# Output-weight parts moved to another pool, and the first stage's pools laid out anew, in a recurrence, attention and expert trunk on one core

## The chip, the cores and the metric

The kernel runs on one core of a Trainium2 chip. TensorE (PE) multiplies matrices, its weight loads are shown apart as PEld; VectorE (DVE), ScalarE (ACT) and GpSimd (POOL) work on tiles; SyncE (SP) issues most DMAs. Each engine runs its own instructions in the order in which the program gives them, and waits for the others by semaphores. The metric is the device time of one execution in microseconds (us), the median of several runs. TensorE's granted clock has two levels here, 1.2 and 2.4 GHz, shown as 0.50 and 1.00.

## What is computed

A trunk of two layers on 256 tokens of width 1024: an RWKV7 layer with a dense SwiGLU, then forgetting attention with a mixture of 8 experts. The change lies in the first, whose time mixing is

```python
r, k, v = jnp.einsum('nbtd,nde->nbte', xs[:3], w_rkv)
...
def step(S, inp):
    r_t, w_t, k_t, v_t, kk_t, a_t = inp
    sa = jnp.einsum('bhij,bhj->bhi', S, -kk_t)
    S = (S * w_t[:, :, None, :] + sa[..., None] * (kk_t * a_t)[:, :, None, :]
         + v_t[..., None] * k_t[:, :, None, :])
    return S, jnp.einsum('bhij,bhj->bhi', S, r_t)
...
y = (y + bonus.reshape(B, T, D)) * g      # y: group norm of the scan's output
return y.astype(x.dtype) @ w_o
```

with 16 heads of 64, followed by `x = x + ...` and a dense stage `silu(u @ w_g) * (u @ w_u) @ w_down` of width 3584.

## The kernel before

Four stages follow each other: `rwkv()` (lines 387 to 1119), `ffn` (the dense stage, line 1122), `fox` and `moe`. Matrices are multiplied in three products: each operand is split into a rounded part and its rest (ACT casts `wh`, DVE subtracts to `wl`, lines 214 to 216), and `mm3` (lines 218 to 221) issues three matmuls.

**The first stage is cut into parts.** The 16 heads are two halves `nh` of 8. Per half: `project` multiplies the mixed inputs by the weights of k, r and v (line 639; v's second half is called the v-projection below); `operands`, `bkt` and `grams` make the scan's operands by chunks of 64 tokens; `solve(nh)` inverts the triangular matrices; `chain(nh, par)` steps the state through 4 chunks, in two parts `par` of four heads each; `finish(nh, t)` does the group norm and the gate for 128 tokens; `outp` multiplies by the output weights. A *group* of `outp` is six matmuls on one output weight and one `t`.

**A solve** writes its diagonal blocks to DRAM (`dU`, line 890) and reads them back turned (`U`, 897), substitutes in 30 steps of two DVE instructions (lines 907 and 909), then two memsets (912, 913), writes the result (`dW`, line 916) and reads it back (lines 921 to 923). Then for two halves `hf`: ACT copy `w11` (line 931), DVE transpose `x11` (933), 16 small matmuls `pB` (938), ACT copy `bsb`, 16 matmuls `pW` (944), ACT copy back. All these DMAs are on SP's queue.

**A chain step** is matmuls `cb` (line 972), ACT copy `rh` (980), matmuls `cc` (984), DVE copy (987), matmuls `ce` (993), two DVE operations (997, 998), matmuls into `cb` (1002) and ACT copy `yt` (1005). The last ones leave in time for the next step.

**`finish`** is three DVE operations (lines 1041 to 1043), ACT square (1046), DVE (1048, 1050), ACT root (1052), DVE (1054 to 1056), four PE transposes (1062), four DVE operations (1066), ACT cast `zh` (1072) and DVE `zl` (1074).

**The order is made by a planner.** The stage's instructions keep the order in which they are written, and `weave` (lines 423 to 496) decides it when the program is built. Every part is a generator that yields an engine and a cost before each piece; `weave` keeps a clock for each engine and goes on with the part whose next piece can start first. A part also waits for marks (`yield "W", ...`) and takes stock: "B" are PSUM banks, "U" small tiles, "Q" the tiles of pool `qpool`, given back by `free`. A rule on a mark or a stock so decides the order of all parts, on all engines.

**Weights.** `loads` brings the 24 weights of k, r, v and the 8 output weights, 512 KB each, on SP's queue through four raw tiles (line 606). `weights` splits those of k and the output weights (lines 630 and 632) into tiles `wh` and `wl` of pool `wsp`, which has two of each:

```python
if len(ns) >= OPT["sb"]:
    yield "W", ("used", ns[-OPT["sb"]])
```

so the split of an output weight waits until `outp` has used the one two before it. The pool `qpool` has 8 tiles of 4 KB per partition; four of them are stock, and hold at the end the recurrence operands `Q`, one for each `nh`, `t` and `par`.

**The dense stage's memory.** After `rwkv()` its pools are freed, and those of the later stages (lines 1667 to 1687) take the same addresses: `fn` (norm tiles, 24 KB per partition), `wraw` (three raw tiles of 8 KB), `wsph` (four of 8 KB), `wspl` (three of 8 KB). `Weights` streams the weights (line 181); it loads and splits ahead where its tiles are free, that is where the tiles of the first stage at the same addresses have been used for the last time. Before, `fn` lies on `rq`, `wraw` on `rq`, `rx` and `rm`, `wsph` on `rm`, `rws` and `ru`, `wspl` on `ru`.

Of the kernel before, what the change touches and what calls it, by code (L numbers as in the profile page):

```python
# [11 lines left out]
F32R = mybir.dt.float32r  # L12
# [95 lines left out]
def tile_trunk(ctx: ExitStack, tc: tile.TileContext, x, norm_g, final_g, mu, w_rkv, w0, w1, w2, a0, a1, a2,  # L108
# [277 lines left out]

    def rwkv():
        es = ExitStack()
        qpool = es.enter_context(tc.tile_pool(name="rq", bufs=8))
        xpool = es.enter_context(tc.tile_pool(name="rx", bufs=2))  # L390
        mpool = es.enter_context(tc.tile_pool(name="rm", bufs=2))
        wsp = es.enter_context(tc.tile_pool(name="rws", bufs=OPT["sb"]))
        upool = es.enter_context(tc.tile_pool(name="ru", bufs=OPT["nu"]))
        lpool = es.enter_context(tc.tile_pool(name="rl", bufs=2))
        wraw = es.enter_context(tc.tile_pool(name="rwr", bufs=4))
        U2 = lambda shape, name, dt=F32: upool.tile(shape, dt, name=name, tag="u")
        h3 = lambda a: a.rearrange("p (h d) -> p h d", d=HD)
        half = lambda c: slice(64 * (c % 2), 64 * (c % 2) + 64)
# [10 lines left out]
        def mark(*key):  # L409
            done[key] = now[0]  # L410

        def free(n, kind):

            stock[kind].extend([now[0]] * n)
# [201 lines left out]
        def weights():  # L616
            ns = []
            for i, key in enumerate(wkey):
                if key in OPT["whole"]:
                    yield "W", ("raw", i)  # L620
                    wts[i] = raw[i], None
                    mark("w", i)
                    continue
                if len(ns) >= OPT["sb"]:
                    yield "W", ("used", ns[-OPT["sb"]])
                ns.append(i)
                yield "W", ("raw", i)
                yield "A", cost_a(1024)
                hi, lo = (wsp.tile([128, 2, 512], F32R, name=nm, tag=nm) for nm in ("wh", "wl"))
                nc.scalar.copy(hi, raw[i])  # L630
                yield "V", cost_v(1024)
                nc.vector.tensor_tensor(lo, raw[i], hi.bitcast(F32), ALU.subtract)
                wts[i] = hi, lo
                mark("rawfree", i)
                mark("w", i)
# [317 lines left out]
        def chain(nh, par):  # L953
            g3 = lambda a: h3(a)[:, par:8:2, :]
            yield "W", ("v", nh)
            for c in range(4):
# [47 lines left out]
                yield "A", cost_a(256), "i"  # L1004
                nc.scalar.copy(g3(y)[half(c)], h3(pb[64:128, 0:256]))
                free(2, "B")
                mark("chain", nh, par, c)
                if last(2, "chain", nh, c):
                    free(3, "U")
# [68 lines left out]
        def outp():  # L1078
# [3 lines left out]
            for i in range(0, 8, 2):  # L1082
# [6 lines left out]
                for t, nh in ((0, 0), (1, 0), (0, 1), (1, 1)) if i < 6 else ((0, 0), (0, 1), (1, 0), (1, 1)):  # L1089
                    yield "W", ("w", n + i + nh)  # L1090
                    yield "P", 1.3
                    for j in range(2):
                        k = i + j
                        mm3(pw[t][nh], zh[k // 4, t][:, k % 4, :], zl[k // 4, t][:, k % 4, :],
                            wts[n + i + nh][0][:, j, :], wts[n + i + nh][1][:, j, :], k == 0, k == KB - 1)
                    if i == 6:
                        yield "V", cost_v(512), "i"
                        add_res(t, nh, pw[t][nh])
                    if t == 1:
                        mark("used", n + i + nh)  # L1100

        gnb = {}
        lwa = lora_w([(w1[0], 3, 0, 64), (a1[0], 4, 64, 64)], "lwa")
# [562 lines left out]
            rwkv()  # L1666
    wes = ExitStack()
    tpool = lambda name, bufs: tc.tile_pool(name=name, bufs=bufs, reuse_waits="tile")
    fpool = wes.enter_context(tpool("fn", 1))
    wraw = wes.enter_context(tpool("wraw", NRA))  # L1670
    specs = []
    if "ffn" in stages:
# [6 lines left out]
    wsp = [wes.enter_context(tpool("wsph", NWH)), wes.enter_context(tpool("wspl", NWL))]  # L1679
    W = Weights([wraw] * NRA, wsp, specs, 2)  # L1680
    W.load()
    mpool = wes.enter_context(tpool("mn", 1))
    wr = mpool.tile([128, KB, E], F32, name="wr")
    load_consts(mpool, C_MOE)
# [75 lines left out]
```

## Time and profile before

| | |
|---|---|
| median of 3 runs | 1637.76 us (1635.51 to 1640.74) |
| the profiled execution's own time | 1641.72 us |
| its span, first to last instruction | 1639.9 us |
| mean granted clock of PE | 0.962 |
| first stage, up to the dense stage's first matmul | 0 to 279.64 us |
| dense stage's first matmul to the end | 279.64 to 1639.9 us |

The profile is of one execution. A timeline row tells when an instruction started, how long it took, and, in brackets, how long its engine had stood idle before it and which instruction of which engine ended that wait. Rows of equal instructions that follow each other are drawn together (x16). In a table by windows the granted clock is a mean over the window: between 0.50 and 1.00 it changed within.

### The profile page before, as it was taken

The page shows a single profiled execution, that of the slowest core. Times are in us where ns is not written, and L with a number is a line of the kernel's source. Part 1 is how long each engine was busy: PE and PEld are TensorE (multiplying, and loading weights), DVE is VectorE, ACT ScalarE, POOL GpSimd, SP SyncE. Part 2 cuts the span into 40 slices and gives each one's busy share as a digit, 9 for nine tenths or more (in the row PEclk, how much of TensorE's full clock was granted, in tenths as well). Part 3 has the DMA queues.
Part 4 walks back from the last instruction along what each step waited for, and adds up shares of the span by engine and source line. Part 5 has one row for each costly group of instructions (what it writes and reads, how often), then busy time and mean ns, then how long its engine had stood idle before and what let it go on. Part 6 is the DMA issues. An engine that isn't in the chain of part 4 may idle for free.

```text
span 1639.9 us, 19904 instructions
## 1 busy us (share of the span) xinstructions
PE 1540.9 (94%) x7309; PEld 1208.2 (74%) x7309; DVE 1275.5 (78%) x1292; ACT 1088.5 (66%) x1092; POOL 176.8 (11%) x230
## 2 busy tenths in 40 slices
PE   5998998999999999999898999999999989989997
PEld 4664876888887886777666788888777667667886
DVE  6587657455536555589999998899799999999986
ACT  4533244444435664489888888787888889887884
POOL 0313010000000000001111111111011111111110
PEclk9997799999999998989999999999999999999999
DMA  5243133554565452369999999899899999999992
GB/s 176 89 110 106 34 104 118 202 204 163 198 196 172 155 180 78 139 262 399 409 403 401 373 395 353 335 394 349 330 382 406 402 403 391 397 402 408 406 359 101
DMA packets 156839, 446.19 MB, mean 272 GB/s; under 512 B 24128, under 2 KB 29296, under 8 KB 156704
## 3 DMA queue, kind: packets, MB, share of 16 engines
q1 hardware_dynamic: 105440, 262.95, 44.2%
q0 software_dynamic: 45920, 176.31, 28.0%
q10 hardware_dynamic: 5344, 5.07, 1.2%
q8 instruction: 91, 1.49, 0.4%
q14 instruction: 44, 0.36, 0.1%
HBM read 442.19 MB, written 2.11 MB: 271 GB/s over the span
## 4 chain that ended last, share of the span: by engine, by line
PE 43%; issue 27%; DMA 9%; DVE 8%; POOL 3%; ACT 3%; POOLq 0%; ACTq 0%; DVEq 0%; SPq 0%
DMA raw<-in_moe_w_gu_dram 9%; PE pgu L1492 8%; POOL raw L181 3%; PE acc L1492 3%; PE pgu L220 3%; PE pgu L221 3%; PE pgu L219 3%; DVE wl L216 3%; ACT wh L215 2%; PE acc L220 2%; PE acc L219 2%; PE acc L221 2%; PE pp L219 1%; PE pp L221 1%; PE pp L220 1%
## 5 line engine op out<-in xcount | busy, mean ns | idle before, releaser
L216 DVE TENSOR_TENSOR wl<-raw,wh 128x2048 fp32r<-128x2048 f32 x398 | 893.9, 2286 | 146.4 <-PE acc L220 35.3
L215 ACT CAST wh<-raw 128x2048 fp32r<-128x2048 f32 x398 | 752.9, 1918 | 272.2 <-PE pgu L221 51.4
L1492 PE MATMUL pgu<-wh,xg 128*128 128x512 f32 x1232 | 329.4, 400 | 1.5 <-issue 1.5
L1492 PEld LDWEIGHTS pgu<-wh,xg 128*128 128x128 f32 x1232 | 237.0, 194 | 52.3 <-issue 2.9
L1492 PE MATMUL pgu<-wl,xg 128*128 128x512 f32 x896 | 252.2, 403 | 10.7 <-DVE wl L216 7.8
L1492 PEld LDWEIGHTS pgu<-wl,xg 128*128 128x128 f32 x896 | 167.6, 192 | 68.2 <-DVE wl L216 35.0
L1492 PE MATMUL acc<-wh,hx 128*128 128x512 f32 x616 | 162.2, 395 | 0.0
L181 POOL DMA_DIRECT2D raw<-in_moe_w_gu_dram x112 | 80.0, 714 | 650.4 <-DVE wl L216 572.2
L1492 PEld LDWEIGHTS acc<-wh,hx 128*128 128x128 f32 x616 | 116.2, 191 | 23.6
L1492 PE MATMUL acc<-wl,hx 128*128 128x512 f32 x448 | 125.4, 401 | 4.5 <-DVE wl L216 2.0
L1492 PEld LDWEIGHTS acc<-wl,hx 128*128 128x128 f32 x448 | 82.6, 190 | 33.9 <-DVE wl L216 17.9
L219 PE MATMUL pgu<-wh,uh 128*128 128x512 f32 x224 | 89.3, 400 | 1.9 <-ACT wh L215 1.9
L220 PE MATMUL pgu<-wl,uh 128*128 128x512 f32 x224 | 88.1, 394 | 1.3 <-DVE wl L216 1.3
L221 PE MATMUL pgu<-wh,ul 128*128 128x512 f32 x224 | 88.1, 394 | 0.0
L181 POOL DMA_DIRECT2D raw<-in_moe_w_down_dram x56 | 39.5, 705 | 271.1 <-DVE wl L216 259.1
L1525 ACT CAST gc<-pgu 128x512 fp32r<-128x512 f32 x112 | 61.1, 594 | 0.0
L1492 PE MATMUL pgu<-gc,fold 128*128 128x512 f32 x70 | 30.9, 480 | 22.2 <-ACT gc L1525 21.9
L220 PEld LDWEIGHTS pgu<-wl,uh 128*128 128x128 f32 x224 | 42.6, 190 | 10.6 <-DVE wl L216 2.0
L219 PEld LDWEIGHTS pgu<-wh,uh 128*128 128x128 f32 x224 | 42.6, 190 | 10.6 <-ACT wh L215 2.1
L221 PEld LDWEIGHTS pgu<-wh,ul 128*128 128x128 f32 x224 | 42.6, 190 | 9.1
L219 PE MATMUL acc<-wh,hh 128*128 128x512 f32 x112 | 43.9, 392 | 0.0
L221 PE MATMUL acc<-wh,hl 128*128 128x512 f32 x112 | 43.7, 390 | 0.0
(361 smaller groups left out, 2013.9 us busy)
## 6 DMA issues: line engine op xcount, KB each, us to landing
raw<-in_moe_w_gu_dram SPq DMA_DIRECT2D x112, 1024.0 KB, 9.9
raw<-in_moe_w_gu_dram POOLq DMA_DIRECT2D x112, 1024.0 KB, 10.2
raw<-in_moe_w_down_dram SPq DMA_DIRECT2D x56, 1024.0 KB, 9.7
raw<-in_moe_w_down_dram POOLq DMA_DIRECT2D x56, 1024.0 KB, 9.6
raw<-in_ffn_w_gu_dram SPq DMA_DIRECT2D x28, 1024.0 KB, 5.5
raw<-in_fox_w_in_dram SPq DMA_DIRECT2D x16, 1024.0 KB, 5.7
raw<-in_ffn_w_down_dram SPq DMA_DIRECT2D x14, 1024.0 KB, 4.9
raw<-in_rwkv_w_rkv_dram SPq DMA_DIRECT2D x24, 512.0 KB, 4.3
```

The source lines that it names most:

```text
L181: (nc.gpsimd if self.nd >= N_EARLY and self.nd % 2 else nc.sync).dma_start(t, src)
L215: nc.scalar.copy(hi, src)
L216: nc.vector.tensor_tensor(lo, src, hi.bitcast(F32), ALU.subtract)
L219: nc.tensor.matmul(o, lh, rh, start=first, stop=False)
L220: nc.tensor.matmul(o, lh, rl, start=False, stop=False)
L221: nc.tensor.matmul(o, ll, rh, start=False, stop=last)
L1492: nc.tensor.matmul(o, l, r, start=first, stop=last, skip_group_check=True)
L1525: nc.scalar.copy(gc, p)
```

## The change

An output weight's `wh` and `wl` now come from `qpool`, in the place of two operand tiles. The split no longer waits for `used`; it takes two "Q" of stock. A "Q" is given back after each second step of a chain part, and two by `outp` after an output weight's last use. The pools of `rwkv` are created in another order, and `fn` after the weights' pools: now `wraw` lies on `rws` and `rx`, `wsph` on `rm` and `rwr`, `wspl` and `fn` on `ru`.

```diff
     def rwkv():
         es = ExitStack()
-        qpool = es.enter_context(tc.tile_pool(name="rq", bufs=8))
+
+        wsp = es.enter_context(tc.tile_pool(name="rws", bufs=OPT["sb"]))
         xpool = es.enter_context(tc.tile_pool(name="rx", bufs=2))
         mpool = es.enter_context(tc.tile_pool(name="rm", bufs=2))
-        wsp = es.enter_context(tc.tile_pool(name="rws", bufs=OPT["sb"]))
+        wraw = es.enter_context(tc.tile_pool(name="rwr", bufs=4))
         upool = es.enter_context(tc.tile_pool(name="ru", bufs=OPT["nu"]))
         lpool = es.enter_context(tc.tile_pool(name="rl", bufs=2))
-        wraw = es.enter_context(tc.tile_pool(name="rwr", bufs=4))
+        qpool = es.enter_context(tc.tile_pool(name="rq", bufs=8))
...
-                if len(ns) >= OPT["sb"]:
-                    yield "W", ("used", ns[-OPT["sb"]])
-                ns.append(i)
+                if key != "o":
+                    if len(ns) >= OPT["sb"]:
+                        yield "W", ("used", ns[-OPT["sb"]])
+                    ns.append(i)
                 yield "W", ("raw", i)
+                if key == "o":
+                    yield "Q", 2
                 yield "A", cost_a(1024)
-                hi, lo = (wsp.tile([128, 2, 512], F32R, name=nm, tag=nm) for nm in ("wh", "wl"))
+                hi, lo = ((wsp if key != "o" else qpool).tile([128, 2, 512], F32R, name=nm, tag=nm if key != "o" else "Q")
+                          for nm in ("wh", "wl"))
...
                 free(2, "B")
+                if c % 2 == 1:
+                    free(1, "Q")
                 mark("chain", nh, par, c)
...
                     if t == 1:
                         mark("used", n + i + nh)
+                        free(2, "Q")
...
-    fpool = wes.enter_context(tpool("fn", 1))
     wraw = wes.enter_context(tpool("wraw", NRA))
...
     W.load()
+    fpool = wes.enter_context(tpool("fn", 1))
```

The planner makes another order from it, from the end of the first solve to the start of the dense stage; from the dense stage's weights on the instructions are in the same order. Line numbers in the changed kernel are higher, by 5 from the weights on, and by 7 from `finish` on. Three places follow.

**SP, the second solve's DMAs and what follows** (`dU`, `U`, `dW`, `Mab` and `w` are the solve's; `raw` are weights). Before:

```order
L890 DMA dU_1256<-Mab 32x32x32 x2
L897 DMA U<-dU_1256 64x1024 x2
L916 DMA dW_1257<-W 1024x1x32 x2
L921 DMA Mab<-dW_1257 32x32x32
L922 DMA w_1594<-dW_1257 32x32x32
L923 DMA Mab<-dW_1257 32x32x32
L606 DMA raw<-in_rwkv_w_o_dram 128x2x512 x7
L181 DMA raw<-in_ffn_w_gu_dram 128x4x512 x28
```

With the change:

```order
L895 DMA dU_1256<-Mab 32x32x32 x2
L902 DMA U<-dU_1256 64x1024 x2
L607 DMA raw<-in_rwkv_w_o_dram 128x2x512 x3
L921 DMA dW_1257<-W 1024x1x32 x2
L607 DMA raw<-in_rwkv_w_o_dram 128x2x512
L926 DMA Mab<-dW_1257 32x32x32
L927 DMA w_1664<-dW_1257 32x32x32
L928 DMA Mab<-dW_1257 32x32x32
L607 DMA raw<-in_rwkv_w_o_dram 128x2x512 x2
L181 DMA raw<-in_ffn_w_gu_dram 128x4x512 x3
L607 DMA raw<-in_rwkv_w_o_dram 128x2x512
L181 DMA raw<-in_ffn_w_gu_dram 128x4x512 x25
```

Three output weights are now issued ahead of `dW`, one between `dW` and the reads that wait for it, and three of the dense stage's weights ahead of the last output weight.

**DVE, the end of the second solve's substitution** (`tm` and `W` are its steps; `VS`, `st` the first chain's). Before, its last steps and what follows:

```order
L907 TENSOR_TENSOR tm<-W,U 128x30
L909 TENSOR_TENSOR W<-W,tm 128x15x2
L907 TENSOR_TENSOR tm<-W,U 128x15
L909 TENSOR_TENSOR W<-W,tm 128x15
L912 MEMSET W 64x16
L913 MEMSET W 64x16
L1041 TENSOR_REDUCE gst<-yt 128x8
L1042 TENSOR_SCALAR gst<-gst 128x8
L1043 TENSOR_TENSOR yt<-yt,gst 128x512
L1048 TENSOR_TENSOR yt<-yt,gnb 128x512
```

With the change, a piece of its middle (the steps of 16 to 14 columns):

```order
L1061 RECIPROCAL gst<-gst 128x8
L1062 TENSOR_TENSOR yt<-yt,gst 128x512
L1063 TENSOR_TENSOR yt<-yt,v_1147 128x512
L912 TENSOR_TENSOR tm<-W,U 128x128
L914 TENSOR_TENSOR W<-W,tm 128x8x16
L992 COPY VS_1169<-cc 64x4x64
L912 TENSOR_TENSOR tm<-W,U 128x120
L914 TENSOR_TENSOR W<-W,tm 128x8x15
L637 TENSOR_TENSOR wl<-raw,wh 128x1024
L912 TENSOR_TENSOR tm<-W,U 128x126
L914 TENSOR_TENSOR W<-W,tm 128x9x14
L1073 SCALAR_TENSOR_TENSOR z<-pz,vt,gT_1351 128x128 x2
```

In all, `finish(0, 0)` from its line 1041 (now 1048) to its line 1074 (now 1081), and one split of an output weight (now line 637), stand within the substitution's steps; before, they stood behind its memsets. The first chain's operations stand within it in both.

**PE, from the second solve's first product on** (`pB`, `pW` are the solve's, `pp` the v-projection, `pwo` a group, `cb` the second chain's first step). Before:

```order
L639 MATMUL pp<-raw,xvh 128x512 x4
L938 MATMUL pB<-x_1655,Mab 32x32 x16
L639 MATMUL pp<-raw,xvh 128x512 x2
L944 MATMUL pW<-w_1594,bsb 32x32 x16
L1062 MATMUL pz<-C_70,yt 128x128 x4
L639 MATMUL pp<-raw,xvh 128x512 x2
L938 MATMUL pB<-x_1729,Mab 32x32 x16
```

and with the change, from the v-projection's last pieces to the solve's first products:

```order
L644 MATMUL pp<-raw,xvh 128x512 x4
L1007 MATMUL cb<-VS_1169,Mrb_628 64x64 x4
L644 MATMUL pp<-raw,xvh 128x512 x2
L977 MATMUL cb<-VS_1174,Q 128x64 x4
L989 MATMUL cc<-rh,Mab 64x64 x4
L1007 MATMUL cb<-VS_1174,Mrb_717 64x64 x4
L1069 MATMUL pz<-C_70,yt 128x128 x4
L943 MATMUL pB<-x_1708,Mab 32x32 x16
L219 MATMUL pwo<-wh,zh_1576 128x512
```

The v-projection's last twelve matmuls stand ahead of `pB` and within the first chain, where before they stood around `pB` and `pW`. Behind these rows, the two groups ahead of the second chain are the same; in that chain before every step holds both parts and one group, and with the change the first step does, the second half of the solve (`pB`, `pW`) follows in the second step, the two parts step one after the other, and one more group stands near the end; the other groups stand behind the chain. On ACT the first three casts of the dense stage's weights now come right behind the last `zh`; on DVE the four additions to `res`, the four `u` and the four `ul` of the dense stage's input now come ahead of its first `wl`, which before stood between the third and the last `ul`.

## Rows read from the trace of the kernel before

**Rows 1.** Page, section 1, in one line (engine, busy time and share of the span, instructions) of the whole span.

```profile
PE 1540.9 (94%) x7309; PEld 1208.2 (74%) x7309; DVE 1275.5 (78%) x1292; ACT 1088.5 (66%) x1092; POOL 176.8 (11%) x230
```

**Rows 2.** Busy time by windows of 5 us: the window, its length, busy time and instructions of PE, PE's weight loads, DVE, ACT and POOL, the granted clock of TensorE as a fraction of its full 2.4 GHz (0.50 is 1.2 GHz), the DMA engines' busy share and GB/s.

```profile
145.00:150.00 5.00, 2.27 (x6) 1.59 (x7) 4.72 (x15) 1.12 (x2) 2.26 (x2) 0.68 0.01 2
...
155.00:160.00 5.00, 5.00 (x10) 2.50 (x10) 2.75 (x6) 0.31 (x1) 0.00 (x0) 0.50 0.84 225
185.00:190.00 5.00, 4.03 (x27) 3.73 (x27) 4.46 (x18) 0.73 (x2) 0.00 (x0) 0.50 0.01 3
195.00:200.00 5.00, 4.74 (x32) 4.43 (x32) 4.51 (x17) 0.73 (x2) 0.00 (x0) 0.50 0.00 0
...
205.00:210.00 5.00, 5.00 (x21) 3.14 (x21) 2.68 (x5) 1.71 (x4) 0.00 (x0) 0.68 0.65 100
275.00:280.00 5.00, 1.98 (x12) 1.33 (x11) 3.87 (x9) 4.47 (x9) 0.00 (x0) 0.99 0.22 59
280.00:285.00 5.00, 3.70 (x9) 2.45 (x8) 5.00 (x5) 3.90 (x4) 0.00 (x0) 0.50 0.37 108
```

**Rows 3.** Timeline of DVE in the second solve and after it: start us, duration us, engine, line, operation, tiles, forms, count, and in brackets idle time before it with what ended it.

```profile
203.98 0.69 DVE L1041 TENSOR_REDUCE gst<-yt 128x8 f32<-128x512 f32 x1
204.70 0.17 DVE L1042 TENSOR_SCALAR gst<-gst 128x8 f32<-128x8 f32 x1
...
210.14 0.69 DVE L1056 TENSOR_TENSOR yt<-yt,v 128x512 f32<-128x512 f32 x1
...
212.18 1.12 DVE L1066 SCALAR_TENSOR_TENSOR z<-pz,vt,gT 128x128 f32<-128x128 f32 x4 [1.02 <-PE pz L1062]
...
217.39 1.22 DVE L632 TENSOR_TENSOR wl<-raw,wh 128x1024 fp32r<-128x1024 f32 x1
...
237.74 0.42 DVE L987 COPY VS<-cc 64x256 f32<-64x256 f32 x1 [2.30 <-PE cc L984]
...
276.37 0.68 DVE L329 TENSOR_TENSOR res<-res,pwo 128x512 f32<-128x512 f32 x1
...
279.62 2.29 DVE L216 TENSOR_TENSOR wl<-raw,wh 128x2048 fp32r<-128x2048 f32 x1 [1.08 <-ACT wh L215]
```

**Rows 4.** Timeline of SP's DMA issues in the two solves (columns as in the group before): the first solve's `dW` at 149.06, the second's at 203.87.

```profile
149.06 1.29 SPq L916 DMA_DIRECT2D dW<-W  x2
150.44 1.30 SPq L606 DMA_DIRECT2D raw<-in_rwkv_w_rkv_dram  x1
157.28 0.33 SPq L921 DMA_DIRECT2D Mab<-dW  x1
...
203.87 1.26 SPq L916 DMA_DIRECT2D dW<-W  x2
207.45 0.31 SPq L921 DMA_DIRECT2D Mab<-dW  x1
...
209.25 34.63 SPq L606 DMA_DIRECT2D raw<-in_rwkv_w_o_dram  x7
```

**Rows 5.** Timeline of ACT: the first copy behind each solve's DMA round trip, and a chain step's copy.

```profile
160.17 0.61 ACT L931 COPY w<-Mab 32x512 f32<-32x512 f32 x1
...
213.86 0.61 ACT L931 COPY w<-Mab 32x512 f32<-32x512 f32 x1
...
249.88 0.37 ACT L980 COPY rh<-cb 64x256 f32<-64x256 f32 x1 [0.67 <-PE cb L972]
```

**Rows 6.** Timeline of PE in the second solve's last part: a piece of the v-projection and the first half's two products.

```profile
206.29 2.90 PE L639 MATMUL pp<-raw,xvh 128*128 128x512 f32 x4
...
216.31 1.19 PE L938 MATMUL pB<-x,Mab 32*32 32x32 f32 x32
...
219.34 1.19 PE L944 MATMUL pW<-w,bsb 32*32 32x32 f32 x32
```

**Rows 7.** Timeline of PE in the chain: the first chain from 183.45 at half clock, and a step of the second at full clock.

```profile
183.45 3.67 PE L972 MATMUL cb<-VS,Q 128*128 128x64 f32 x16
...
189.99 1.97 PE L993 MATMUL ce<-VS,BK 128*64 128x64 f32 x16 [0.97 <-DVE VS L987]
...
193.79 3.67 PE L972 MATMUL cb<-VS,Q 128*128 128x64 f32 x16
...
228.34 1.89 PE L972 MATMUL cb<-VS,Q 128*128 128x64 f32 x16
...
235.03 2.00 PE L972 MATMUL cb<-VS,Q 128*128 128x64 f32 x16
...
238.14 0.50 PE L219 MATMUL pwo<-wh,zh 128*128 128x512 f32 x1
...
239.73 1.15 PE L993 MATMUL ce<-VS,BK 128*64 128x64 f32 x16
...
241.88 2.00 PE L972 MATMUL cb<-VS,Q 128*128 128x64 f32 x16
```

**Rows 8.** Timeline of PE at the end of the first stage and the start of the dense one.

```profile
260.81 0.50 PE L220 MATMUL pwo<-wl,zh 128*128 128x512 f32 x1 [0.18 <-DVE wl L632]
...
270.80 0.50 PE L220 MATMUL pwo<-wl,zh 128*128 128x512 f32 x1 [0.48 <-DVE wl L632]
...
279.64 1.03 PE L219 MATMUL pgu<-wh,uh 128*128 128x512 f32 x2 [1.89 <-ACT wh L215]
281.97 0.80 PE L220 MATMUL pgu<-wl,uh 128*128 128x512 f32 x1 [1.30 <-DVE wl L216]
```

## The prediction

> **What bounds the kernel now.** I read the page first: over the whole span PE is busy 94% [rows 1], so what a stage costs is mostly what PE does in it and how fast. Then the busy time in windows over the first stage, because there the granted clock is not the same throughout [rows 2]. The reader is to see three things. Where PE was nearly empty (2.27 of 5 us busy at 145 to 150, 1.98 at 275 to 280), the windows behind stand at 0.50. The fall is not undone by any work: at 155 to 160 PE is shown busy for all of 5.00 us and still stands at 0.50, and under the first chain, with 4.03 to 4.74 us busy in each window, it stays there. And in 205 to 210, where the v-projection's wide matmuls start [rows 6], the mean is 0.68, so the clock came back within that window. DVE meanwhile is busy 4.46 to 4.51 of 5 us in the second solve's substitution [rows 2].
>
> Then the order of the waits about the second solve. Its substitution ends on DVE with the issue of `dW` at 203.87; the reads go out at 207.45; the first copy behind them is at 213.86 [rows 4, 5]. While the solve is on its way to DRAM and back, PE has the v-projection, and between `pB` and `pW` as well [rows 6]. The second chain starts at 228.34 and runs at full clock [rows 7]. At the end PE waits for the split of output weights twice (0.18 and 0.48 us), for the first dense cast 1.89 us and for the first dense `wl` 1.30 us [rows 8]. The first stage ends in a chain of such waits; what happens there shifts everything behind it by as much.
>
> **(a) The substitution.** Into it move seven DVE operations of 512 columns at 0.69, two small ones at 0.17, the four of `z` at 1.12 together and one split at 1.22: 7 × 0.69 + 2 × 0.17 + 1.12 + 1.22 = 7.5 us [rows 3]. DVE is the engine that sets the substitution's pace, so I take all of it: `dW` goes out at 211.4. The idle time left to DVE is about 0.5 us in each of four windows [rows 2], so the least is 5.5. At most the moved operations also make DVE wait once, as for `z` or the chain, some 2 us more. That `finish(0, 0)` is then done sooner gains nothing, since the chain behind it hangs on the solve.
>
> **(b) From `dW` to the second chain.** In the second solve `dW` to the copy takes 213.86 − 203.87 = 10.0; in the first solve, where SP issues one weight between `dW` and the reads, the reads wait until 157.28, 8.2 us behind `dW` in the place of 3.6, and the copy is at 160.17, 11.1 us behind it [rows 4, 5]. The change has the first solve's order, so I take 11.1. The least is the quick reads of the one and the short rest of the other, 3.6 + 2.9 = 6.5. On SP the last output weight now stands behind three dense weights, whose tiles come free only with the solve's second half; only the last groups want it, behind the chain, so I cost that at nothing, and without that cover PE would wait there as it waits for a split now [rows 8]. The Trainium skill ("DMA: Bandwidth & Descriptors", section "Queues, rings and completion order") says that on each DMA engine the descriptors of one queue are consumed in ring order, so that a weight issued behind `dW` would not hold it up. By that the trip would be 6.5 and the sum 4.6 lower; the 8.2 us of the first solve speak against it.
>
> Copy to `pB` is 2.45; from `pB` to `pW` it was 3.03, with a v-projection piece between; a group (239.73 − 238.14 = 1.59 [rows 7]) stands there now, so I take 2.6; then `pW` 1.19 and a second group 1.59 [rows 5 to 7]. So the second chain starts at 211.4 + 11.1 + 2.45 + 2.6 + 1.19 + 1.59 = 230.3, against 228.34: **+2.0** for (a) and (b) together at full clock. The ends are −4.6 (5.5 and 6.5 taken) and +4.0.
>
> **(c) The second chain, at full clock.** A step takes 241.88 − 235.03 = 6.85 with its group [rows 7]. Now its two parts no longer step together, and the solve's second half stands in it. Each time that a part steps alone, one ACT copy of 0.37 and three DVE operations of 0.42 are not covered by the other part [rows 3, 5]: 1.6 us a step, at most 4 × 1.6 = 6.5. The least is nothing, if the out-projection's groups, which move behind the chain, would have taken the time anyway. I take **+5**, near the upper end, since groups no longer fill the last three steps.
>
> **(d) The end of the stage.** The output weights are split ahead, and the dense casts too: waits of 0.18, 0.48 and 1.89 go, **−2.5** [rows 8]. At best the 1.30 goes too (−3.9), at worst none.
>
> **(e) The first dense `wl`.** Before, it started 279.62 − 276.37 = 3.25 us behind the last addition to `res` [rows 3]. Now four `u` and four `ul`, 512 columns each, stand between: 8 × 0.69 = 5.5, with the addition itself 6.2. That is **+2.9**; the least is 0, if PE has other work.
>
> At full clock the sum is 2.0 + 5 − 2.5 + 2.9 = **+7.4**; the ends are −4.6 + 0 − 3.9 + 0 = −8.5 and +13.4.
>
> **(f) The clock.** With the v-projection ahead of the solve's return, PE has only the first chain's last pieces and four transposes from about 207 to `pB` at 225: more emptiness than in either of the two windows behind which the clock fell [rows 2]. So I expect 0.50 from there, and then only narrow work with a few groups, as under the first chain, where it did not come back. The first chain's step at half clock is 193.79 − 183.45 = 10.34, of which 0.97 is a wait for a busy DVE: 9.4 [rows 7]. Without its group a full-clock step is 6.85 − 1.59 = 5.3, so a step costs 4.1 more, 16.4 for four; PE is then what sets the pace, so (c) is within it and not added. Three groups double, 3 × 1.59 = 4.8, and so do `pB` and `pW` of the first half, 2.4. With the clock back in the wide matmuls that follow the chain, the sum is 2.0 + 16.4 + 4.8 + 2.4 − 2.5 + 2.9 = **+26.0**.
>
> The sum is against the profiled execution, 1641.72 us, whose span is 1639.9 and which lies 4 us above the median of 1637.76. So 1667.7 for such an execution, and **1663.8** as a median. About 0.3% (4.9 us) is what a measurement of this kernel tells from no change: the same is 1632.9 to 1642.7.
>
> **The rivals.**
>
> *The clock stays or comes back early.* Two groups stand ahead of the chain, and the v-projection brought the clock back within one window. Then only the full-clock sum counts, with a part of (f) at the start: +7.4 to +14, 1645 to 1652. For it: 205 to 210 [rows 2]. Against it: 155 to 160, where 5 us of busy PE were not enough. By the Trainium skill ("TensorE: Matmul & The Clock Gate", section "What's actually happening") the throttle is released by sustained activity, which would be this case; the windows of the first chain, busy and at 0.50, do not bear it out for narrow matmuls.
>
> *Faster: the moved work fits into idle time.* DVE takes 2 of the 7.5 us in gaps, the trip is the short one of 6.5, PE is not short of work for long enough that its clock falls, the groups moved behind the chain fill what was waiting, and all four waits at the end go: −8.5, 1629. It decides if `dW` goes out before about 209.5 and the second chain starts before 226 at full clock. Against it: a DVE busy nine tenths, and the first solve's slow trip.
>
> *The half clock lasts through the out-projection.* Thirteen groups stand behind the chain's first step; at half clock they take up to 13 × 1.59 = 21 longer, of which I take half, since their wide matmuls are what brings it back: about +10 more, 1674. For it: 155 to 160.
>
> *No effect.* What is moved fills gaps and what is lost is won at the end, so that −8.5 and +7.4 meet: 1633 to 1642.
>
> **How the numbers follow.** The forecast, half clock through the second chain: 0.5 (1653 to 1670). Early return: 0.18 (1645 to 1652). Half clock for longer: 0.1 (1674). Faster: 0.12 (1629). No effect: 0.1. So slower 0.78, the same 0.1, faster 0.12. The predicted time is the likeliest case's, 1664. The range takes in the first three cases and the upper edge of the fourth: 1641 to 1676; outside it stay the faster case and most of no effect.
>
> **What would show it.** In the changed kernel's windows: 0.50 or a fall to it about 210 to 225, and steps of some 9.4 us in the second chain. On SP `dW` at about 211 and the read behind it 8 us later. On DVE the first dense `wl` with eight operations of 0.69 between it and the last addition. On PE no wait for the split of an output weight. The prediction is wrong if the second chain's steps are at 1.00, or if `dW` goes out before 209, or if PE still has wide matmuls when the solve returns; and its size is wrong if the trip is 6.5 or the clock comes back only in the dense stage.

## The result, and the profile after

| | before | with the change |
|---|---|---|
| median | 1639.25 us (1635.51 to 1642.38, 4 runs) | 1664.56 us (1661.01 to 1667.28, 4 runs) |
| ratio | | 1.0148, 95% interval 1.0112 to 1.0183 |
| the profiled execution's time, span | 1641.72, 1639.9 us | 1661.01, 1659.2 us |
| mean granted clock of PE | 0.962 | 0.959 |

The change makes the kernel 25 us slower (18 to 30 by the interval). All of it that the two profiles show arises before the dense stage has its first split weight. To see where, I cut the stretch at four marks that every kernel of this study has: the first step of the second solve's substitution (DVE), its `dW` (SP), the second chain's first `cb` (PE), the chain's last `yt` (ACT), and the dense stage's first matmul on `wl` (PE). Since the marks are in the same run, the table is free of what happens ahead of them; the substitution started between 180 and 194 us in the runs of this study, with no edit there in most of them.

| us, one profiled execution each | substitution | `dW` to chain | chain | chain to dense | sum |
|---|---|---|---|---|---|
| before | 20.2 | 24.5 | 24.8 | 28.8 | 98.3 |
| with the change | 29.5 | 18.7 | 40.2 | 30.4 | 118.8 |

The marks that no other row shows, before (DVE, ACT) and with the change (DVE, ACT):

```profile
183.63 0.19 DVE L907 TENSOR_TENSOR tm<-W,U 128x30 f32<-128x30 f32 x1 [0.64 <-ACT W L899]
253.14 0.37 ACT L1005 COPY yt<-cb 64x256 f32<-64x256 f32 x1 [0.21 <-PE cb L1002]
183.69 0.43 DVE L912 TENSOR_TENSOR tm<-W,U 128x30 f32<-128x30 f32 x1
272.08 0.37 ACT L1010 COPY yt<-cb 64x256 f32<-64x256 f32 x1 [3.16 <-PE cb L1007]
```

The substitution takes 9.3 longer, the way from `dW` to the chain 5.8 less, the chain 15.4 more and the rest 1.6 more: 20.5. The spans differ by 19.3, so what follows gives no part of it in this pair. The medians differ by 25; the profiled execution of the changed kernel is the fastest of its four, so some 5 us of the loss are in no profile. One run of e3 below (1666.31 us) counts as slow, being over 1.5% above the fastest, and is left out of e3's figures.

**The clock.** Busy time by windows of the changed kernel (columns as in [rows 2]):

```profile
210.00:215.00 5.00, 1.61 (x16) 1.28 (x15) 3.34 (x13) 0.04 (x1) 1.96 (x5) 0.74 0.11 18
215.00:220.00 5.00, 0.00 (x0) 0.00 (x0) 4.17 (x8) 2.31 (x4) 0.00 (x0) 0.50 0.89 191
225.00:230.00 5.00, 5.00 (x55) 3.90 (x53) 0.11 (x1) 0.58 (x1) 0.00 (x0) 0.55 0.00 0
230.00:235.00 5.00, 5.00 (x53) 4.55 (x51) 2.34 (x3) 2.88 (x5) 0.00 (x0) 1.00 0.02 3
240.00:245.00 5.00, 4.94 (x81) 4.62 (x78) 1.25 (x3) 1.22 (x3) 0.61 (x1) 0.81 0.39 103
245.00:250.00 5.00, 4.15 (x26) 3.64 (x25) 0.42 (x1) 0.73 (x2) 0.00 (x0) 0.50 0.99 378
265.00:270.00 5.00, 5.00 (x23) 4.16 (x23) 2.15 (x6) 0.99 (x2) 0.00 (x0) 0.50 0.00 0
275.00:280.00 5.00, 5.00 (x18) 3.90 (x18) 4.93 (x8) 2.11 (x3) 0.00 (x0) 0.77 0.00 0
```

PE is all but empty from 210 to 225, and the clock falls to 0.50, as it did behind [rows 2]'s empty windows. It is back within 225 to 230. Then it falls again in 240 to 245, with PE shown busy for 4.94 of 5 us, and stays at 0.50 until 275 to 280. So in this execution the second chain loses its clock while it runs, not from what came before.

**PE about the chain** (timeline, columns as in [rows 3]):

```profile
224.39 1.91 PE L943 MATMUL pB<-x,Mab 32*32 32x32 f32 x32 [1.82 <-DVE x L938]
226.24 0.80 PE L219 MATMUL pwo<-wh,zh 128*128 128x512 f32 x1
...
229.09 1.34 PE L949 MATMUL pW<-w,bsb 32*32 32x32 f32 x32
...
231.87 1.89 PE L977 MATMUL cb<-VS,Q 128*128 128x64 f32 x16
...
238.56 1.10 PE L977 MATMUL cb<-VS,Q 128*128 128x64 f32 x8
...
242.58 0.68 PE L998 MATMUL ce<-VS,BK 128*64 128x64 f32 x8
243.19 1.97 PE L977 MATMUL cb<-VS,Q 128*128 128x64 f32 x8
...
247.05 1.11 PE L989 MATMUL cc<-rh,Mab 64*64 64x64 f32 x8 [0.85 <-ACT rh L985]
...
253.77 1.97 PE L977 MATMUL cb<-VS,Q 128*128 128x64 f32 x8
```

Behind one group of wide matmuls at half clock (226.24 to 229.09) the clock is back: the second product runs mostly at full clock, and the chain's first step (231.87 to 238.56, 6.7 us, as in [rows 7]) wholly. At 243.19 eight `cb` take 1.97 us in the place of 1.10, with no wait of PE ahead of them. The later `cc` of 8 matmuls takes 1.11 us in the place of 0.67, with waits of 0.85 for ACT in between.

**The solve** (timelines of SP and ACT):

```profile
213.19 1.26 SPq L921 DMA_DIRECT2D dW<-W  x2
214.90 0.37 SPq L607 DMA_DIRECT2D raw<-in_rwkv_w_o_dram  x1
217.29 0.33 SPq L926 DMA_DIRECT2D Mab<-dW  x1
```

```profile
220.68 0.62 ACT L936 COPY w<-Mab 32x512 f32<-32x512 f32 x1 [1.04 <-DMA Mab<-dW]
```

`dW` goes out at 213.19. A weight is issued behind it, as in the first solve of [rows 4], but the read that waits for `dW` goes out 4.1 us behind it, not 8.2, and the copy starts 7.5 us behind it. From the read to the copy it is 3.4 us, where it was 6.4 in [rows 4, 5]. Before, ACT had two operations ahead of the copy, one of them behind a wait of 3.64 us for PE, and the copy followed the second without a wait of its own:

```profile
213.34 0.62 ACT L1072 CAST zh<-z 128x512 fp32r<-128x512 f32 x1 [0.19 <-DVE z L1066]
```

So a part of the 10.0 us before was the order on ACT, not the way to DRAM and back.

**DVE in the substitution, and POOL beside it** (timelines):

```profile
208.16 0.24 DVE L912 TENSOR_TENSOR tm<-W,U 128x78 f32<-128x78 f32 x1
208.43 0.96 DVE L914 TENSOR_TENSOR W<-W,tm 128x78 f32<-128x78 f32 x1
209.43 0.95 DVE L912 TENSOR_TENSOR tm<-W,U 128x65 f32<-128x65 f32 x1
...
210.93 0.52 DVE L914 TENSOR_TENSOR W<-W,tm 128x56 f32<-128x56 f32 x1
```

```profile
208.25 2.05 POOL L701 TENSOR_TENSOR v<-v,bs 128x512 f32<-128x512 f32 x2 [17.83 <-ACT v L685]
...
210.77 1.19 POOL L982 TENSOR_TENSOR sp<-VS,PC 64x256 f32<-64x256 f32 x2
```

POOL's two `bonus` multiplications, which came behind the substitution before, now run within it. Two DVE steps of 0.24 us take 0.95 and 0.96 while they last. The next two beside POOL's products of 256 columns (`sp`, of the second chain) take 0.52 and 0.53 in the place of 0.22 and 0.20: 2.1 us in four operations. e1, e4 and e5 below show the same four.

**The end** (DVE, then PE):

```profile
294.73 0.69 DVE L329 TENSOR_TENSOR res<-res,pwo 128x512 f32<-128x512 f32 x1 [1.14 <-PE pwo L221]
295.33 2.48 DVE L286 TENSOR_TENSOR u<-ptr,vt 128x512 f32<-128x512 f32 x4
297.72 2.49 DVE L216 TENSOR_TENSOR ul<-u,uh 128x512 fp32r<-128x512 f32 x4
...
300.19 2.29 DVE L216 TENSOR_TENSOR wl<-raw,wh 128x2048 fp32r<-128x2048 f32 x1
```

```profile
296.80 1.83 PE L219 MATMUL pgu<-wh,uh 128*128 128x512 f32 x4 [0.67 <-ACT uh L215]
302.53 0.80 PE L220 MATMUL pgu<-wl,uh 128*128 128x512 f32 x1 [3.90 <-DVE wl L216]
```

Four `u` (2.48 us) and four `ul` (2.49) stand between the last addition and the first dense `wl`, which starts 5.5 us behind the addition, against 3.25 in [rows 3]. PE waits 3.90 for it, against 1.30 in [rows 8]; the wait for the first `wh` (1.89) and those for an output weight's split are gone.

### The profile page after: what moved, and what is told of

Its sections match the earlier page's. It is cut to its first block, busy times and chain, and to the rows that moved or that the text cites. A ratio compares the mean times of both kernels' runs of the same rounds, so it can differ in the third digit from the quotient of the medians.

```text
span 1659.2 us, 19888 instructions
## 1 busy us (share of the span) xinstructions
PE 1541.9 (93%) x7309; PEld 1207.0 (73%) x7309; DVE 1277.5 (77%) x1292; ACT 1092.5 (66%) x1092; POOL 175.9 (11%) x230
## 4 chain that ended last, share of the span: by engine, by line
PE 41%; issue 27%; DMA 10%; DVE 9%; POOL 3%; ACT 2%; POOLq 0%; DVEq 0%; ACTq 0%; SPq 0%
DMA raw<-in_moe_w_gu_dram 9%; PE pgu L1500 7%; POOL raw L181 3%; DVE wl L216 3%; PE acc L1500 3%; PE pgu L220 3%; PE pgu L221 3%; PE pgu L219 3%; PE acc L220 2%; PE acc L219 2%; PE acc L221 1%; PE pp L219 1%; PE pp L220 1%; PE pp L221 1%; ACT wh L215 1%
## 5 line engine op out<-in xcount | busy, mean ns | idle before, releaser
L1500 PEld LDWEIGHTS acc<-wl,hx 128*128 128x128 f32 x448 | 82.6, 190 | 33.1 <-DVE wl L216 17.0
```

The source lines that it names most:

```text
L1500: nc.tensor.matmul(o, l, r, start=first, stop=last, skip_group_check=True)
```

## The experiments

Two theories at the start: the order that the planner makes puts the second chain at half clock (mine), or the longer substitution and the uncovered round trip make up the loss. Each median stands beside the runs of the kernel before on the same chip. This is the table above for all of them:

| run | median (before) | ratio, 95% | substitution | to chain | chain | to dense |
|---|---|---|---|---|---|---|
| e1 tiles only | 1666.5 (1638.5) | 1.0095 to 1.0187 | 29.5 | 20.5 | 41.0 | 30.0 |
| e2 pools only | 1644.2 (1638.5) | 1.0002 to 1.0068 | 20.2 | 24.8 | 24.8 | 33.1 |
| e3 first in wsp | 1649.7 (1638.5) | 1.0029 to 1.0096 | 20.3 | 23.7 | 26.2 | 31.6 |
| e4 both halves | 1672.5 (1638.5) | 1.0144 to 1.0226 | 34.4 | 27.3 | 34.4 | 31.2 |
| e5 filler | 1662.5 (1639.2) | 1.0127 to 1.0220 | 34.3 | 18.7 | 35.0 | 29.9 |
| e6 no groups | 1653.9 (1639.2) | 1.0056 to 1.0121 | 20.8 | 22.6 | 36.2 | 34.9 |
| e7 finish held | 1669.1 (1639.2) | 1.0130 to 1.0217 | 27.1 | 21.1 | 45.7 | 31.6 |
| e8 last two | 1647.3 (1639.2) | 1.0030 to 1.0076 | 20.2 | 24.3 | 24.8 | 26.1 |
| e9 v held | 1667.5 (1638.8) | 1.0143 to 1.0194 | 21.2 | 43.3 | 30.7 | 33.7 |
| e10 before, filled | 1642.2 (1638.8) | 0.9991 to 1.0040 | 20.4 | 25.0 | 24.8 | 28.8 |
| e11 v and finish held | 1660.8 (1638.5) | 1.0078 to 1.0198 | 25.5 | 23.1 | 48.2 | 29.6 |
| e12 v held later | 1659.4 (1638.5) | 1.0069 to 1.0202 | 37.5 | 23.0 | 24.8 | 31.2 |

### Which part of the change: e1 and e2

**e1** leaves the pools where they were and `fn` ahead of `wraw`.

> The change's tile part alone (output-weight parts in the operands' tiles, with the stock rules), on the pools' old layout. The planner's order is then the changed kernel's up to the dense stage. If the loss lies in the order (my theory): 1657 to 1670, as the changed kernel. If a part of it lies in the layout of the pools: below 1652.

1666.5: the tile part alone gives the whole loss, and nearly the same table.

**e2** has only the lines of the diff on the pools' order and `fn`.

> The pools' new layout alone, with the old tiles and the old rule. PE's order in the first stage is the one before. Theory: the first dense casts come earlier, so that the wait of 1.9 us for the first one may go; 1634 to 1640, no measurable loss. Rival, the layout makes a tile wait for a late reader of the old pool: over 1645.

1644.2, a small loss that neither guess held. Up to the chain's end nothing changes; behind it 4.3 us are lost. Timelines of SP and of ACT:

```profile
220.24 34.74 SPq L606 DMA_DIRECT2D raw<-in_rwkv_w_o_dram  x7
287.12 10.55 SPq L181 DMA_DIRECT2D raw<-in_ffn_w_gu_dram  x4
```

```profile
293.05 1.90 ACT L215 CAST wh<-raw 128x2048 fp32r<-128x2048 f32 x1 [2.19 <-DMA raw<-in_ffn_w_gu_dram]
```

The dense stage's first weights now lie on the pool `rws`. Without the tile part the output weights' parts are still in it, so the loads go out at 287.12, behind the last use, where before they went out behind the last output weight at 243.94; the first dense cast waits 2.19 us for one. The layout needs the tile part, and together they do give the early casts, the first at 282.39. They gain nothing at this end: in e1, without the layout, the first dense cast starts at 300.22, and from the chain to the dense stage it takes 30.0 as against 30.4.

### What makes the order: e3

```diff
-                if key != "o":
+                early = key != "o" or i < len(wkey) - 8 + 1
+                if early:
```

and `early` decides the pool and the stock in the lines that follow.

> The changed kernel, but the first output weight's parts stay in the old two-tile pool; the other seven take operand tiles. The planner's order is then the one before up to the second solve (v-projection about the solve's round trip, finish behind the substitution, both parts of the second chain in step), but only one output group stands within the second chain. If the loss comes from the order ahead of the second chain: 1632 to 1640. If it comes from a second chain without wide matmuls, whose clock falls: at 4.1 us for each step at half clock, two to four of them, 1645 to 1655.

1649.7, more than half of the loss gone by one tile. The first output weight was cast on ACT at 171.64, ahead of the first chain's second steps; in the changed kernel it waits for a "Q" of that chain and is cast at 190.25 (172.72 here), and the planner takes another way through everything behind. With that weight in the old pool the substitution (20.3) and the way to the chain (23.7) are as before. The chain, with both parts in step and one group in it, runs two steps of 5.4 us at 1.00 in the profiled run, falls to 0.50 in its third and takes 26.2. The fall comes with a wait of PE, 13 us behind the chain's start at 228.04, and no group stands in those 13 us:

```profile
242.16 1.97 PE L990 MATMUL cc<-rh,Mab 64*64 64x64 f32 x16 [1.30 <-ACT rh L986]
```

The group from 244.06 to 246.99 runs at half clock, and by 248.82 the clock is back. The runs spread from 1640 to 1658; I take this to be the chain's clock, which one profile can't show.

### The chain's clock: e6, e5, e11, e12, e4

**e6** is the kernel before with

```diff
                 if pw is None:
+                    yield "W", ("chain", 1, 0, 3), ("chain", 1, 1, 3)
                     yield "B", 4
```

> The kernel before, but the output projection starts only when the second chain is done: both parts still step together, ahead of it nothing changes, and the six groups ahead of and within the chain move behind it. PE's work is the same. If the chain needs the groups for its clock, it falls within it: steps of 9 to 10 us in the place of 5.3 for one to three of them, 1643 to 1656. If not, the chain takes 21 to 22 us in the place of 24.8 and the groups come behind it: 1635 to 1642.

The last windows ahead of the chain and at its start, then the chain's starts on PE:

```profile
220.00:225.00 5.00, 4.14 (x64) 2.75 (x63) 2.42 (x6) 4.07 (x8) 0.00 (x0) 0.97 0.46 163
225.00:230.00 5.00, 5.00 (x36) 4.82 (x35) 0.00 (x0) 2.72 (x6) 2.61 (x3) 0.50 1.04 385
```

```profile
225.56 3.67 PE L972 MATMUL cb<-VS,Q 128*128 128x64 f32 x16
...
234.86 3.67 PE L972 MATMUL cb<-VS,Q 128*128 128x64 f32 x16
...
244.15 3.67 PE L972 MATMUL cb<-VS,Q 128*128 128x64 f32 x16
...
254.52 3.67 PE L972 MATMUL cb<-VS,Q 128*128 128x64 f32 x16
```

Steps of 9.3 and 10.4 us, the whole chain at 0.50, though both parts step together and PE is nearly always busy: 36.2 us in the place of 24.8, with the five groups ahead of it and in it moved behind it (not six, as I had counted; the chain's fourth step has no group before, though the section on the change has one in every step). So without the five the chain does not run at 1.00. But the clock falls at about 225, ahead of the chain and not within it, behind a wait of PE of 0.66 us where a group had stood. Whether the two groups ahead of the chain or the three in it keep the clock in the kernel before, this run doesn't separate.

**e5** adds to the changed kernel, in the same order, ahead of the `cc` matmuls

```diff
                 pcm = ps("cc")
+                if nh == 1 and c > 0:
+                    for _ in range(3):
+                        nc.tensor.matmul(pcm[64:128, 256:512], ident[:, 0:64], res[0][:, 0:256], start=True, stop=True,
+                                         skip_group_check=True)
```

> The changed kernel, in the same order, with three matmuls more (64 rows, 256 columns) ahead of each cc of the second chain from its second step on; they write a part of the bank that nobody reads and use a wait for ACT. Seven part steps, some 1.5 us of work each. If the half clock makes the second chain long (40 us in the changed kernel, 25 before), the clock now stays at 1.00 and the chain takes 26 to 32 us in spite of the added work; 1650 to 1657. If the parts' stepping alone makes it long, it takes 40 to 48 us; 1664 to 1672.

Windows:

```profile
185.00:190.00 5.00, 5.00 (x35) 4.82 (x32) 2.90 (x13) 1.31 (x3) 0.56 (x1) 0.50 0.00 0
...
250.00:255.00 5.00, 5.00 (x50) 3.99 (x48) 1.22 (x3) 1.31 (x3) 0.61 (x1) 1.00 0.74 249
260.00:265.00 5.00, 5.00 (x44) 3.77 (x44) 4.85 (x10) 1.92 (x5) 0.00 (x0) 1.00 0.20 59
```

```profile
246.98 1.51 PE L990 MATMUL cc<-res,C 128*64 128x256 f32 x6
```

The chain is at 1.00 throughout (two of its windows above) and takes 35.0 in the place of 40.2, in spite of 6 × 1.51 = 9.1 us of added matmuls (the edit gives six part steps, not the seven that I had expected). PE is shown busy for 34.4 of the 35.0 us, so without the filler the same order at full clock would take between 25.9 and 35.0, by my estimate from these figures; of the 15.4 us, the clock is 5.2 at least and 14.3 at most. This is the profile of the fastest of four runs, which spread from 1653.6 to 1676.5; whether the clock stayed in the others isn't shown. The chain's time is a miss (I had said 26 to 32), and so is the median. In the profiled run the filler costs most of what the clock gives: the sum of the four stretches is 117.9, against 118.8. The substitution, 34.3 here and 29.5 in the changed kernel in the same order, stood at half clock at its start (first window); in the changed kernel it was at 1.00. With the v-projection in it, its length went with PE's clock (e4, at half, took 34.4; e1, at 1.00, 29.5). Before, DVE set it: 20.2 at 0.50.

**e11 and e12** let the last three quarters of the v-projection's second half wait for the substitution's end,

```diff
                 for i in range(4):
+                    if (key, nh, i) == ("v", 1, 1):
+                        yield "W", ("sub", 1)
```

and e11 the two finishes of the first half as well (`if nh == 0: yield "W", ("sub", 1)`); `mark("sub", nh)` stands behind the substitution's loop.

> The changed kernel, but the last three quarters of the v-projection's second half and both finishes of the first head half wait for the end of the second solve's substitution. The v-projection covers the round trip again, three groups stand ahead of the second chain and six within it, but its parts still step one after the other. If wide matmuls in the chain are what it needs: clock at 1.00 through the chain, 26 to 31 us for it with its six groups, substitution 20 to 23, total 1638 to 1646. If the stepping of the parts one after the other is what makes the chain long: 35 us or more, total 1650 or more.

> As the run before it, but the finishes are not held: now both of them and a split stand in the second solve's substitution, twice the moved DVE work of the changed kernel. Both parts of the second chain step together, with groups in their first steps, and the v-projection covers the round trip. If each moved finish costs its DVE time in the substitution: 20.2 + 7 + 6.5, so 33 to 36 us for it, and the chain 24 to 28 us at 1.00; total 1650 to 1658. If DVE has room there: the substitution takes under 28 us, total under 1646.

Windows over the chain, of e11 and then of e12:

```profile
235.00:240.00 5.00, 4.28 (x38) 3.39 (x35) 2.39 (x4) 2.16 (x4) 1.38 (x1) 1.00 1.02 379
240.00:245.00 5.00, 4.89 (x38) 4.54 (x39) 1.25 (x3) 0.43 (x2) 0.16 (x1) 0.54 1.05 394
245.00:250.00 5.00, 5.00 (x23) 3.73 (x21) 0.95 (x3) 0.37 (x1) 0.62 (x1) 0.50 0.15 52
```

```profile
245.00:250.00 5.00, 5.00 (x51) 4.32 (x50) 2.43 (x5) 1.68 (x3) 0.00 (x0) 1.00 1.05 394
250.00:255.00 5.00, 5.00 (x55) 4.60 (x53) 2.37 (x6) 2.42 (x5) 1.23 (x2) 1.00 0.50 184
255.00:260.00 5.00, 5.00 (x54) 4.36 (x52) 3.33 (x6) 1.51 (x4) 1.97 (x2) 1.00 0.00 0
```

e11 is a miss against my theory as I had put it there: five groups within the chain (not six, as I had counted), and the clock still falls in 240 to 245; 48.2 us. Its parts step one after the other. e12's parts step together with groups in the first two steps: 1.00 throughout, 24.8 us. In e11, moreover, a group at half clock (245.42 to 248.28) is not followed by 1.00, nor are the next two (the fourth is); the `ce` behind the first still takes 1.12 us in the place of 0.68:

```profile
248.28 1.12 PE L1001 MATMUL ce<-VS,BK 128*64 128x64 f32 x8
```

So the chains that were at 1.00 from end to end are those in the order before (e2, e8 and e10 too) and e12's, with both parts in step and groups among them, and e5's, with its added matmuls. Why the clock falls where it does stays open. In e3, e4, e6, e9 and e11 it fell at a wait of PE of 0.52 to 1.57 us; in the changed kernel it fell without one; and e12's chain had a wait of 0.86 and kept it. e12's substitution took 37.5 us with two finishes and a split in it, 17.3 more than before; their DVE operations are 2 × 6.3 + 1.2 = 13.8, and DVE is busy 30.9 of the 37.4 us. So the moved finishes cost their DVE time and some waits.

**e4** lets the second chain wait for both halves of the solve (`yield "W", ("solve", nh, 3 if nh else c)`).

> The changed kernel, but the second chain starts only when both halves of the second solve are done; its parts then step together again, with groups in the first three steps, and the order ahead of it stays the changed one. The chain starts some 6 us later. If the chain's half clock is the loss, steps of 6.9 us at full clock instead of about 10.5, less the later start: 1648 to 1656. If the longer substitution and the round trip are the loss: 1663 to 1672.

1672.5, worse than the change. The chain took 34.4 in the place of 40.2, at 1.00 for two steps and falling in the third (0.70 in 270 to 275), but started 8.6 later behind `dW`, and the substitution, at half clock in this run, took 34.4. The numbers fit the rival's, for another reason: what the chain gained, the later start and the substitution took.

### Putting pieces back, and a version that might win: e7, e9, e8, e10

**e7** lets `finish(0, 0)` alone wait for `("sub", 1)`.

> The changed kernel, but the first finish waits for the end of the second solve's substitution, as in the order before. The substitution then takes about 20 to 22 us in the place of 29.5, and dW goes out 7 to 9 us sooner. The second chain stays without groups and its parts step alone. If the length of the substitution is what counts: 1650 to 1656. If the second chain's clock is: a part of those us only, since one group less stands ahead of the chain and the clock is lower from the start: 1656 to 1664.

1669.1. The substitution fell to 27.1 only: at half clock DVE waits 2.98 and 2.03 us in it for the first chain's matmuls, which stand among the v-projection's. The chain, without the group that the early finish had allowed and at 0.50 from its start, takes 45.7.

**e9** holds the v-projection's whole second half.

> The changed kernel, but the v-projection's second half waits for the end of the second solve's substitution, so that it covers the solve's round trip again. The planner then puts both parts of the second chain in step, four groups ahead of and in its first step and one in each of the next two. If the move of the v-projection out of the round trip is what cost the time (PE empty, clock lost, chain unpaired): substitution about 20 us, second chain 24 to 27 us at 1.00, total 1638 to 1646. If the loss is in the tiles or the layout: 1655 or more.

A miss of the edit: before, a quarter of it ran ahead of the substitution; now all of it came behind, and `dW` to chain took 43.3. The substitution was back at 21.2.

**e8** gives operand tiles to the last two output weights alone, lays `rws` and `rq` last, and splits the first dense weights ahead of the norm (`with tc.high_priority(offset=2 * AHEAD): W.split_ahead()`).

> Only the last two output weights take operand tiles, the other six stay in the old pool with the old rule; that pool and the operands' lie last, so that the dense stage's first tiles overlay neither; the dense weights' first splits are put ahead of the norm's. PE's order is the one before to the end of the second chain, so its clock should be too; at the end of the stage the waits for a split (0.48), for the first dense cast (1.9) and for the first dense wl (1.3) should go: 2 to 5 us less than before, 1633 to 1637. If the order at the end makes a new wait: 1638 to 1645.

The profiled run, of 1640.35 us, has the shortest stage of all, 95.4, with 2.7 us gained at the end; but the median is 1647.3. The runs reach from 1639 to 1656, and where the slower ones lose it isn't shown.

**e10** is the kernel before with matmuls added where PE stood empty.

```diff
+            if nh == 1 and o:
+                for _ in range(3):
+                    nc.tensor.matmul(pa, ident, res[0][:, 0:512], start=True, stop=True)
```

and four of the same into `pgu[0][0]` ahead of the dense stage's first.

> The kernel before with added matmuls (128 by 512, results overwritten) where PE stands empty and the clock falls behind it: three ahead of each of the two last transposes of P (130.39 and 147.73 in its trace), four ahead of the dense stage's first matmul. If the lost clock costs time there: the v-projection at 148 to 160 and the first 7 us of the dense stage run at 1.00, 3 to 7 us less, 1631 to 1636, and a fast second solve's start in most runs. If other engines bound these stretches: no difference, 1637 to 1641; if the added work is in the way: up to 6 us more.

1642.2, no difference that can be told. The windows from 145 to 160 and from 280 to 290 were at 1.00 in its profile, but the clock fell at 160 to 165, and the stretch from the substitution on takes 99.0 us, as against 98.3; what was saved was not kept. None of the versions beat the kernel before.

## Why the prediction was right, point by point

The forecast, slower by 26 through a lost clock, held: 25, and 1664.6 against 1663.8. The sum is better than its terms. It was worked out for the profiled execution, as 1667.7, and that one took 1661.0, with 20.5 us in the four stretches; that the medians agree to 0.8 us is luck in part.

- **(a), the substitution: mechanism right, too small.** 9.3 for 7.5. The 2.1 us that DVE lost beside POOL's `bonus` and `sp` were not in the sum; I had followed the v-projection on PE but not what its end lets start on POOL. That the substitution would hang on PE's clock (29.5 or 34.3) I did not see either.
- **(b), the round trip: wrong price.** I took 11.1 from the first solve, where a weight stood between `dW` and the reads; it was 7.5, near the low end of 6.5 (e4 7.2 in the same order). The Trainium skill ("DMA: Bandwidth & Descriptors", "Queues, rings and completion order") says that each DMA engine consumes a queue's descriptors in ring order. The second solve agrees: a load issued behind `dW` on the same queue held up the read by no more than 0.5 us (4.1 against 3.6; 4.5 in e4). What held up the first solve (8.2 before, 6.8 with the change) isn't shown. And the 10.0 us of the second solve before were in part the order on ACT, as said above.
- **(f), the price of the clock: near in sum, wrong in its course.** The clock did fall where PE stood empty, in 210 to 215. But it was back at 230 behind one group, so I had the fall that counted at the wrong place: it came at 243, in the chain. That the groups and `pB`, `pW` would double was half true (`dW` to chain came to 18.7, where the sum had 18.9 at full clock and 24.5 with two groups and the products at half). The chain's 15.4 was put at 16.4, for four steps at half clock; the first ran at 1.00, which was one of the signs of being wrong, and e5 gives the clock 5.2 to 14.3 of the 15.4. That the two figures are so near is luck in part.
- **(c), the parts stepping alone,** I had dropped at half clock as covered. e11, with this stepping and groups, lost its clock; e5, with this stepping and the added matmuls, kept it. So the stepping does not decide the clock by itself. What share of 15.4 it has by its own waits stays open: e5 leaves 25.9 to 35.0 for the order at full clock.
- **(d) and (e), the end:** 0.4 forecast, 1.6 measured. The early casts came, and the wait for `wl` grew by 2.6.
- **The rivals.** Early return: the clock did come back early and then left again, so its condition held and its time did not. The Trainium skill's sentence that sustained activity releases the throttle ("TensorE: Matmul & The Clock Gate", "What's actually happening") agrees with the group at 226 to 229; the chain of e6, busy and at 0.50 for 36 us, and the three groups of e11 that 1.00 did not follow do not bear it out. Half clock through the out-projection: it was at 1.00 from 280 to 295. Faster: neither of the two signs that decide it was there (`dW` at 213, chain at 231.9).

## What to carry to other kernels

When a planner writes the order, a changed rule on one tile is a change of the whole order behind it: compare the orders of all engines before costing the edit (one output weight's wait decided more than half of this loss). Read PE's granted clock beside its busy share, because narrow matmuls can show a busy PE at half clock. In this kernel wide independent matmuls about and among the narrow steps of a recurrence were worth their place (without them the chain took 11.4 us more, e6), and the chains that kept their clock without added work had two independent parts in step (before, e12). And a memory layout made for one change can cost without it (e2): run the parts apart.

## What had not been expected of the hardware

- One group of six matmuls of 512 columns at half clock (226.24 to 229.09) was followed by 1.00, and so was one in e3 (244.06 to 246.99); three such groups in e11 were not. Chains of 64-column matmuls with PE shown 4.2 to 5.0 of 5 us busy stayed at 0.50 for 30 us and more.
- Beside two POOL multiplications of 512 columns (2.05 us), two DVE operations of some 0.24 us took 0.95 and 0.96; beside two of 256 columns (1.19), two of 0.22 and 0.20 took 0.52 and 0.53.
- The second substitution started at 182.1 us in e6 and at 194.4 in e2, with the order ahead of it that of the kernel before in both. Of the 12.3 us, 5.5 were there at the start of the first substitution (110.99 and 116.53), with the clock at 1.00 in both up to 110. In the rest the clock differed: 0.82 and 0.86 in e6 from 170 to 180 and from 180 to 190, 0.50 in e2. That is a reason to compare stretches within a run.
